# A two-layer trunk on one core: value and solution rows in one tile, products over 128 rows, small work off GpSimd, one projection a period ahead

## The chip, the cores and the metric

The kernel runs on one core of a Trainium2 chip. The metric is the device time of one execution in microseconds, the median of several runs. The engines are named as the profile names them: PE (TensorE, matrix products; PEld is its weight load), DVE (VectorE), ACT (ScalarE), POOL (GpSimd) and SP (SyncE, which issues most transfers). Each engine works through its own list of instructions in order and waits on semaphores for the others.

## What is computed

A trunk of two layers over 640 tokens (128 of a prompt, 512 of a sample, 1024 channels), with a norm and a conditioning in front of each layer and a last norm. The first layer holds a gated convolution and a bidirectional RWKV-7 recurrence over 16 heads of 64 channels; the second is gated linear attention. The change is in the first layer's recurrence and in what runs around it:

```python
def _wkv7_scan(r, w, k, kk, a, v, s0):
    def step(s, inp):
        r_t, w_t, k_t, kk_t, a_t, v_t = inp
        s_kk = jnp.einsum('zbhvk,zbhk->zbhv', s, kk_t)
        s = (s * w_t[..., None, :] - s_kk[..., :, None] * (kk_t * a_t)[..., None, :]
             + v_t[..., :, None] * k_t[..., None, :])
        return s, jnp.einsum('zbhvk,zbhk->zbhv', s, r_t)

w_raw = w0 + einsum(tanh(h @ w1), w2)                 # low-rank decay, two directions
decay = jnp.exp(-jnp.exp(-jax.nn.softplus(-w_raw) - 0.5))
o, s_fin = _wkv7_scan(r, decay, k_mod, kk, iclr, v, s0)   # forward and backward
gn = group_norm(o_fwd + o_bwd)
bonus = jnp.sum(rh[None] * k_mod * r_k, axis=(0, -1))[..., None] * vh
o_wkv = (gn + bonus) * jax.nn.silu(zw)
y = jnp.concatenate([o_conv, o_wkv], axis=-1) @ w_out
```

## The kernel before, in words

**Dense products.** Every projection (each head pair has its own 1024x128 block of every weight) is made as 128x320 products of split operands: each weight tile is split into a high part (ACT, L330) and a rest (POOL, L333), and three products hi·hi, lo·hi and hi·lo are summed. One projection is 48 such products of 320 tokens. In the rows they are `pd_...<-hi,hi_...`.

**The recurrence in chunks of 64 tokens.** Heads go in pairs, eight pairs, and each pair has its *period*. A period holds eight chain steps (`chain_step`, s = 0 to 7); a step treats two or three lanes (a lane is one chunk of one direction; 20 lanes a period, of which 18 update the state) for both heads h. A step has three stages on PE with `gap()` called twice behind each:

1. `x_mm` and `v_mm`: the right-hand side from the state X and the values V, into the PSUM tile `pa`; ACT copies it to `rh` (L994). Beside it POOL makes XP, the decayed state (L989).
2. `kv_mm`, `q_mm`, `gv_mm`: what V and X give to the new state and to the output, into `pu`; `t_mm`: the solution, from `rh`, into `pa`; ACT copies it with a minus to U (L1020).
3. `bk_start` (transposes of the next step's keys, copied to `bkt` by ACT, L941), then `bu_mm` and `gu_mm`: what U gives to state and output. DVE makes the new X (L1034), and the output goes to `oac` (L948 to L954).

V of head h lies in partitions HS[h], U of head h in the other half, HB[h], and all products of a step contract over 64 rows.

**What fills the gaps.** `Period.__call__`, run at every gap (48 a period), issues dense products by a quota and the small work (`Work`) that is due at this gap by the table PR: `p_lr` (low-rank decay of the pair after next: lw, ta), `p_kk` and `p_kb`, `expand_all` of the next pair (exponentials Pq and iP on ACT, products `ar` and `bk` on DVE L766 to L790, the pG products on PE and their masking on DVE L804), `inv_a` and `inv_b` (the triangular inversion, with a store to DRAM and a load), `vrows`, `bonus` (L856, L857), and of the pair before `fin_b` (DVE L1082) and `fin_t` (transposes pgn). `Work(p, g, n, first, last, ns, need)` spreads n pieces over the gaps first to last. The planner orders instructions on each engine by the priority in force when they were issued (PRE, CH, EV, FIN, BG).

**Period 7** has no next pair. Its dense work is the convolution's output projection (eoc), and DVE computes the second layer's conditioning (`gemv`, L247, into gacc; `gemv_cols` turns it to columns by one-column products pmod on PE).

In the table `en` a letter names the engine of each of twelve products E(0) to E(11): V is DVE and G is POOL.

Of the kernel before, what the change touches and what calls it, by code (L numbers as in the profile page):

```python
# [9 lines left out]
PR = {'NC0': 8,  # L10
# [16 lines left out]
 'ib': [42, 45],  # L27
# [5 lines left out]
 'ex': [1, 16],  # L33
 'inv': 17,
 'vr': 26,
 'bo': [28, 30],
 'lr': [34, 41],
 'kk': [40, 42],
 'init': 40,
 'fb': 10,  # L40
 'ft': [13, 16],
 'kb': [45, 46],
# [12 lines left out]
 'en': 'VVVVVGVVGVVV',  # L55
# [17 lines left out]
 'ex6': [1, 16],  # L73
 'inv6': 17,
# [3 lines left out]
 'fb6': 10,  # L78
 'ft6': [13, 16],
# [8 lines left out]
 'g49': [14, 39],  # L88
# [10 lines left out]
P = 128  # L99
# [28 lines left out]
def tile_trunk(ctx, tc, A, O):  # L128
# [318 lines left out]


# [216 lines left out]
    def p_lr(hp):  # L665
        w2h, w2l = {}, {}

        def load(i):
            w2 = wp.tile([P, 2, P], F32, tag="w2", name=f"w2_{hp}_{i}")
            nc.sync.dma_start(w2, A["w2"][hp, :, i])  # L670
            w2h[i] = wp.tile([P, 2, P], F32R, tag="w2h", bufs=2, name=f"w2h_{hp}_{i}")
            x = S.activation(w2h[i], w2, AF.Copy)
            if hp == 0 and i == 1:
                tc.keep_in_program_order(x)
            return w2

        def low(i, w2):

            w2l[i] = wp.tile([P, 2, P], F32R, tag="w2l", name=f"w2l_{hp}_{i}")
            G.tensor_tensor(w2l[i], w2, w2h[i].bitcast(F32), op=ALU.subtract)  # L680
        low(1, load(1))
        raw0 = load(0)
        yield 0
        lw, ta = [], []
        for (lst, i, boff, tg) in ((ta, 1, 16, "ta"), (lw, 0, 0, "lw")):
            if not i:
                low(0, raw0)
                lwt = el.tile([P, 2, TOK], F32, tag="lw", name=f"lw{hp}")
            for d in range(2):
                o = et(f"{tg}{d}", f"{tg}{hp}_{d}") if i else lwt[:, d]  # L690
                b = der[:, boff + d * 8 + hp:boff + d * 8 + hp + 1]
                for s in range(2):
                    ps = pm(f"plr{hp}_{d}_{tg}_{s}")
                    t = slice(s * HT, (s + 1) * HT)
                    mm(ps[:, 0:HT], w2h[i][:, d], hlr[i, d][:, t], start=True, stop=False)
                    mm(ps[:, 0:HT], w2l[i][:, d], hlr[i, d][:, t], start=False, stop=True)
                    evict(lambda: S.activation(o[:, t], ps[:, 0:HT], AF.Tanh, scale=0.5, bias=b))
                    yield 270
                lst.append(o)
        for d in range(2):  # L700
            S.activation(lw[d], lw[d], AF.Identity, scale=-0.5 * CW, bias=mcw)
            for t in (slice(0, HT), slice(HT, TOK)):
                m, x = cc("sm", HT, d), lw[d][:, t]
                if d == 1:
                    m, x = m[:, ::-1], x[:, ::-1]
                V.tensor_tensor_scan(x, m, x, 0.0, op0=ALU.mult, op1=ALU.add)
        st[hp].update(lw=lw, ta=ta)

    def p_kk(hp):
# [4 lines left out]
        for t in (slice(0, HT), slice(HT, TOK)):  # L714
            S.activation(kk[:, t], k[:, t], AF.Square, scale=pc("kk", hp))
# [31 lines left out]
    def expand(hp, d, c0):  # L747
# [16 lines left out]
        if d == 0:  # L764
            E(11).tensor_tensor(ar[:, :, 1, 1:], kk3[:, :, 1:], P3[:, :, :-1], op=ALU.mult)
            V.tensor_copy(ar[:, :, 1, 0:1], kk3[:, :, 0:1])  # L766
            end = P3[:, :, C - 1]
            if c0 == 0:
                V.tensor_copy(PC[:, 0:2, 2], end[:, 0:2])
                V.tensor_copy(PC[:, 0:3, 0], end[:, 2:5])  # L770
            else:
                V.tensor_copy(PC[:, 3:8, 0], end)
        else:
            E(11).tensor_tensor(ar[:, :, 1, 1:][:, :, ::-1], kk3[:, :, :-1], P3[:, :, 1:], op=ALU.mult)
            V.tensor_copy(ar[:, :, 1, 0:1], kk3[:, :, C - 1:C])
# [16 lines left out]
    def pairs(hp, d, c0, m):  # L792
# [100 lines left out]
    def inv_b(hp):  # L893
# [3 lines left out]
        T = et("r", f"Tb{hp}").rearrange("p (c x) -> p c x", x=B)  # L897
# [23 lines left out]
    def chain_init(hp):  # L921
# [3 lines left out]
        oac = wk.tile([P, NCH, 64], F32, tag="oac", bufs=2, name=f"oac{hp}")  # L925
        st[hp]["X"], st[hp]["oac"] = X, oac
# [29 lines left out]
    def chain_step(hp, s, gap):  # L956
# [12 lines left out]
        if s == 0:  # L969
            bk_start(hp, 0, ta)  # L970
# [18 lines left out]
        dict(V=V, G=G)[PR["xpc"]].tensor_tensor(XP[:, l0:nl], X[:, l0:nl], PC[:, s, l0:nl].unsqueeze(2).to_broadcast([P, nl - l0, 64]), op=ALU.mult)  # L989
# [7 lines left out]

        begun = set()

        def kv_mm(l, d, c, h):  # L1000
            mm(po[HS[h], 0, l], bt[HS[h], l, 64 * h:64 * h + 64], Vt[HS[h], c], start=h not in begun, stop=False, skip_group_check=True)
            begun.add(h)

        def q_mm(l, d, c, h):
            if full(l):
                mm(po[HS[h], 1, l], ar[HS[h], d, c, 0], X[HS[h], l], start=False, stop=False, skip_group_check=True)

        def gv_mm(l, d, c, h):
            mm(po[HS[h], 1, l], Gt[h][HS[h], d, c, 0:C], Vt[HS[h], c], start=False, stop=False, skip_group_check=True)
# [112 lines left out]
    class Work:  # L1122
# [147 lines left out]
    def period(hp):  # L1270
# [7 lines left out]
        if n < NHP:  # L1278
# [4 lines left out]
            misc += [Work(PRE, expand_all(n), 8, *(PR["ex" + z] if hp else PR["ex0"]), 540, (n, "r"))]  # L1283
# [620 lines left out]
```

## Time and profile before

| what | value |
|---|---|
| median of 3 runs | 1467.71 us (1459.54 to 1475.93) |
| the profiled execution | 1467.22 us |
| its span | 1465.5 us |
| mean granted clock of PE | 0.944 |
| busy: PE, DVE, ACT, POOL | 92%, 67%, 43%, 35% |
| periods | eight, about 107 us each, from 191.5 to 1070 us; period 7 from 943 us |

A busy share is over the whole span. The page's chain of work that ended last goes by PE for 45% and by DVE for 34%. The stages differ: inside a period there is a stretch in which the next pair's operands are expanded, with other limits than the rest, so the periods are read by windows below. A record is what the profiler logs; one product of 64x64 in 32 bits shows as two records.

### The profile page before, as it was taken

Reading aid. Unit: us, or ns where it says so; the run is one execution under the profiler, and the core shown is the slowest. Engines: PE = TensorE matmul, PEld = TensorE weight load, DVE = VectorE, ACT = ScalarE, POOL = GpSimd, SP = SyncE. Lnnn points to the kernel's source line nnn. Section 1 sums busy time; section 2 is a strip of 40 time slices with the busy share of each in tenths; the row PEclk is TensorE's granted clock in tenths of the full one; section 3 lists DMA queues with packets and bytes.
Section 4 is the critical chain, followed back from the end, with each engine's and each line's share of the span. In section 5 each row is a group of like instructions: output and inputs, shape, how many; then the busy total and the mean of one; then the engine's idle time right before and its main releaser. Section 6 shows DMA issues by size and latency. Waiting matters only on the chain.

```text
span 1465.5 us, 34615 instructions
## 1 busy us (share of the span) xinstructions
PE 1353.6 (92%) x13495; PEld 1240.8 (85%) x13495; DVE 981.3 (67%) x2283; ACT 630.8 (43%) x1574; POOL 519.3 (35%) x675
## 2 busy tenths in 40 slices
PE   9889899999999999898999989888999999999997
PEld 4779788888888888887888878878989888999997
DVE  4386556785876786685686787675775687746454
ACT  4543253454444444444444533442344664344341
POOL 1433233323323333233223223443355444343332
PEclk9989999999999999899999989997889999999998
DMA  9112212212212212212212212455544321422143
GB/s 367 38 51 82 78 45 66 71 39 74 65 46 63 66 50 65 56 42 72 56 43 71 64 55 62 118 184 165 163 116 131 110 72 53 124 73 89 56 130 102
DMA packets 139636, 127.28 MB, mean 87 GB/s; under 512 B 54096, under 2 KB 121936, under 8 KB 139472
## 3 DMA queue, kind: packets, MB, share of 16 engines
q1 hardware_dynamic: 136912, 118.38, 27.3%
q0 software_dynamic: 2016, 6.16, 1.1%
q8 instruction: 106, 1.74, 0.5%
q14 instruction: 58, 0.48, 0.1%
q10 hardware_dynamic: 544, 0.52, 0.1%
HBM read 108.37 MB, written 16.65 MB: 85 GB/s over the span
## 4 chain that ended last, share of the span: by engine, by line
PE 45%; DVE 34%; DMA 7%; issue 4%; POOL 3%; ACT 2%; SPq 0%; DVEq 0%; POOLq 0%; ACTq 0%
DVE Ai L881 6%; DVE Ai L879 6%; PE pd_oo L135 3%; PE pd_zg L135 3%; PE pu L135 3%; PE pd_eoc L135 3%; PE pd_gb L135 3%; PE pd_r L135 3%; DVE bk L790 3%; PE pd_v L135 3%; PE pd_qk L135 2%; PE pd_vg L135 2%; DVE bk L787 2%; DMA gw<-in_ada_dram 2%; PE pd_u L135 2%
## 5 line engine op out<-in xcount | busy, mean ns | idle before, releaser
L879 DVE TENSOR_TENSOR Ai<-Ai 80x30 f32<-80x30 f32 (+14 forms) x240 | 96.5, 402 | 22.8 <-DMA Ai<-Ad 15.5
L881 DVE TENSOR_TENSOR Ai<-Ai 80x30 f32<-80x30 f32 (+14 forms) x240 | 100.1, 417 | 6.9
L135 PE MATMUL pG<-ar,bk 64*128 64x128 f32 x640 | 66.4, 320 | 27.7 <-DVE G L804 15.3
L135 PEld LDWEIGHTS pG<-ar,bk 64*128 64x128 f32 x640 | 52.3, 212 | 40.4 <-DVE G L804 17.2
L804 DVE TENSOR_TENSOR G<-pG,con 128x512 f32<-128x512 f32 (+1 forms) x96 | 53.1, 594 | 26.1 <-PE pG L135 25.8
L247 DVE SCALAR_TENSOR_TENSOR gacc<-gw,cf,gacc 128x512 f32<-128x512 f32 x70 | 59.9, 895 | 15.3 <-DMA gw<-in_ada_dram 15.1
L1034 DVE SCALAR_TENSOR_TENSOR X<-pu,PC,XP 128x64 f32<-128x64 f32 x144 | 33.1, 275 | 51.9 <-POOL lo_k L333 27.6
L989 POOL TENSOR_TENSOR XP<-X,PC 128x128 f32<-128x128 f32 (+2 forms) x56 | 30.3, 542 | 101.0 <-DVE X L1034 85.5
L333 POOL TENSOR_TENSOR lo_eoc<-wr_eoc,hi_eoc 128x256 fp32r<-128x256 f32 x48 | 40.2, 846 | 50.9 <-ACT hi_eoc L330 30.9
L333 POOL TENSOR_TENSOR lo_r<-wr_r,hi_r 128x256 fp32r<-128x256 f32 x32 | 25.2, 791 | 82.0 <-ACT hi_r L330 81.4
L1020 ACT ACTIVATE U<-pa 128x192 f32<-128x192 f32 (+1 forms) x64 | 19.3, 302 | 77.9 <-PE pa L135 77.9
L994 ACT ACTIVATE rh<-pa 128x192 f32<-128x192 f32 (+1 forms) x64 | 19.2, 300 | 65.5 <-PE pa L135 65.5
L135 PE MATMUL pd_eoc<-hi,hi_eoc 128*128 128x320 f32 x128 | 45.5, 356 | 1.0 <-ACT hi_eoc L330 1.0
L135 PE MATMUL pd_eoc<-hi,lo_eoc 128*128 128x320 f32 x128 | 44.0, 343 | 2.5 <-POOL lo_eoc L333 2.5
L790 DVE TENSOR_TENSOR bk<-ta,iP 64x320 f32<-64x320 f32 x64 | 44.4, 693 | 1.4
L135 PE MATMUL pd_gb<-hi,hi_gb 128*128 128x320 f32 x128 | 43.4, 339 | 0.7 <-DVE cy L619 0.7
L135 PE MATMUL pd_eoc<-lo,hi_eoc 128*128 128x320 f32 x128 | 43.4, 339 | 0.4 <-POOL lo L1207 0.4
L135 PE MATMUL pd_gc<-hi,hi_gc 128*128 128x320 f32 x128 | 43.7, 342 | 0.0
L135 PE MATMUL pd_gc<-hi,lo_gc 128*128 128x320 f32 x128 | 43.7, 341 | 0.0
L135 PE MATMUL pd_gc<-lo,hi_gc 128*128 128x320 f32 x128 | 43.2, 338 | 0.0
L135 PE MATMUL pd_r<-hi,hi_r 128*128 128x320 f32 x128 | 42.3, 331 | 0.6 <-ACT hlr L583 0.6
L135 PE MATMUL pd_gb<-hi,lo_gb 128*128 128x320 f32 x128 | 42.4, 331 | 0.0
(484 smaller groups left out, 5096.8 us busy)
## 6 DMA issues: line engine op xcount, KB each, us to landing
gw<-in_ada_dram SPq DMA_DIRECT2D x64, 256.0 KB, 3.1
gw<-in_ada_dram SPq DMA_DIRECT2D x16, 512.0 KB, 8.6
wr_eoc<-in_eo_dram SPq DMA_DIRECT2D x48, 128.0 KB, 2.8
wr_qk<-in_ow_dram SPq DMA_DIRECT2D x33, 128.0 KB, 2.2
wr_r<-in_ew_dram SPq DMA_DIRECT2D x32, 128.0 KB, 2.4
wr_v<-in_ew_dram SPq DMA_DIRECT2D x32, 128.0 KB, 2.2
wr_u<-in_ew_dram SPq DMA_DIRECT2D x32, 128.0 KB, 2.2
wr_gc<-in_ew_dram SPq DMA_DIRECT2D x32, 128.0 KB, 2.2
```

The lines of the kernel that those rows point to most:

```text
L135: tc.keep_in_program_order(T.matmul(*a, **kw))
L247: V.scalar_tensor_tensor(acc[j], w, c, acc[j], op0=ALU.mult, op1=ALU.add)
L333: le.tensor_tensor(lo, w, hi.bitcast(F32), op=ALU.subtract)
L787: V.scalar_tensor_tensor(x if d == 0 else x[:, :, ::-1], b13[HS[h]], 0.5, iP3[HS[h]], op0=ALU.mult, op1=ALU.mult)
L790: E(2).tensor_tensor(bk[HS[h], :, h], ta3[HS[h]], iP3[HS[h]], op=ALU.mult)
L804: V.tensor_tensor(q["G"][h][:, d, c0:c0 + m], ps[h][:, 0:P * m].rearrange("p (c x) -> p c x", x=P), cc("mk", P, 256 * h + P * d).unsqueeze ...
L879: V.tensor_tensor(tt, Ai[:, 0:i, i:i + 1].to_broadcast([80, i, n]), Ai[:, i:i + 1, i + 1:].to_broadcast([80, i, n]), op=ALU.mult)
L881: V.tensor_tensor(Ai[:, 0:i, i + 1:], Ai[:, 0:i, i + 1:], tt, op=ALU.add)
L989: dict(V=V, G=G)[PR["xpc"]].tensor_tensor(XP[:, l0:nl], X[:, l0:nl], PC[:, s, l0:nl].unsqueeze(2).to_broadcast([P, nl - l0, 64]), op=ALU.mult)
L994: S.activation(rh[:, 0:nl], pr[:, 0:nl], AF.Copy)
L1020: S.activation(U[:, 0:nl], pr[:, 0:nl], AF.Copy, scale=-1.0)
L1034: V.scalar_tensor_tensor(Xn[:, l], po[:, 0, l], PC[:, s, l:l + 1], XP[:, l], op0=ALU.mult, op1=ALU.add)
```

## The change

**One tile for V and U.** A step now has a tile VU with V of head h in partitions HS[h] and minus the solution in HB[h]. ACT copies V's part (two operations, four where a step has three lanes) and writes the solution's part in two operations of 64 partitions. `kv_mm` and `bu_mm` become one `s_mm`, `gv_mm` and `gu_mm` one `o_mm`, both contracting over 128 rows, both in stage 3.

**Work off GpSimd and DVE.** XP is made by ACT, one operation a lane. The products E(5) (gn by sz) and E(8) (the bonus) go from POOL to DVE. The ten small copies a pair in the expansion (L766 to L781) go from DVE to ACT.

**Places.** The projection r of a pair is made a period earlier (at the end of the dense list; v stands first). `inv_b` keeps its T in the tile that will be `oac`, no longer in r's. The transposes for step 0 of the next pair are issued in step 7 of this one. `p_lr(0)` starts ahead of ten dense products in the prologue. The table's gaps change: expansion [1, 16] to a list of eight gaps, inversion 17 to 14, `fin_b` 10 to 14 and `fin_t` 13-16 to 17-20, `p_lr` 34-41 to 39-47, `p_kk` 40-42 to 38-40, `ib` 42-45 to 44-47, `gemv_cols` [14, 39] to [18, 46]; `Work` accepts a list of gaps. `fin_s` goes from priority EV+600 to PRE+100, `load_wkv(0)` from BG to EV, and the squares of kk are issued through `evict`.

```diff
- 'ex': [1, 16],
+ 'ex': [0, 1, 5, 7, 9, 11, 12, 13],
- 'en': 'VVVVVGVVGVVV',
+ 'en': 'VVVVVVVVVVVV',
...
-            V.tensor_copy(ar[:, :, 1, 0:1], kk3[:, :, 0:1])
+            S.activation(ar[:, :, 1, 0:1], kk3[:, :, 0:1], AF.Copy)
...
-        T = et("r", f"Tb{hp}").rearrange("p (c x) -> p c x", x=B)
+        oac = st[hp]["oac"] = wk.tile([P, NCH, 64], F32, tag="oac", bufs=2, name=f"oac{hp}")
+        T = oac.rearrange("p a x -> p (a x)").rearrange("p (c x) -> p c x", x=B)
...
-        if s == 0:
+        if s == 0 and hp == 0:
             bk_start(hp, 0, ta)
...
-        dict(V=V, G=G)[PR["xpc"]].tensor_tensor(XP[:, l0:nl], X[:, l0:nl], PC[:, s, l0:nl].unsqueeze(2).to_broadcast([P, nl - l0, 64]), op=ALU.mult)
+        for l in range(l0, nl):
+            S.activation(XP[:, l], X[:, l], AF.Copy, scale=PC[:, s, l:l + 1])
...
+        VU = wk.tile([P, 2, 3, 64], F32, tag="VU", name=f"VU{hp}_{s}")
+        a, b = 2 + s, 9 - s
+        for h in range(2):
+            if a < b:
+                S.activation(VU[HS[h], h, 0:2], Vt[HS[h], a:b + 1:b - a], AF.Copy)
...
+            if nl == 3:
+                S.activation(VU[HS[h], h, 2], Vt[HS[h], lanes[2][2]], AF.Copy)
...
-        each(kv_mm, upd)
         each(q_mm, lanes)
-        each(gv_mm, lanes)
         each(t_mm, lanes)
         gap()
         gap()
-        U = wk.tile([P, 3, 64], F32, tag="U", name=f"U{hp}_{s}")
-        S.activation(U[:, 0:nl], pr[:, 0:nl], AF.Copy, scale=-1.0)
...
-        bk_start(hp, s + 1, ta)
-        each(bu_mm, upd)
-        each(gu_mm, lanes)
+        for h in range(2):
+            S.activation(VU[HB[h], h, 0:nl], pr[HB[h], 0:nl], AF.Copy, scale=-1.0)
+
+        def s_mm(l, d, c, h):
+            mm(po[HS[h], 0, l], bt[:, l, 64 * h:64 * h + 64], VU[:, h, l], start=False, stop=False, skip_group_check=True)
+
+        def o_mm(l, d, c, h):
+            mm(po[HS[h], 1, l], Gt[h][:, d, c, 0:C], VU[:, h, l], start=False, stop=l == nl - 1, skip_group_check=True)
+        if s < 7 or hp < 7:
+            bk_start(hp + s // 7, (s + 1) % 8, ta)
+        each(s_mm, upd)
+        each(o_mm, lanes)
...
-            dense_ += [(PRE, p_r(n)), *conv_next(a), (PRE, p_v(n)), *conv_next(b)]
+            dense_ += [(PRE, p_v(n)), *conv_next(a)]
...
-                dense_ += [(PRE, p_k(n + 1))]
+                dense_ += [(PRE, p_k(n + 1)), *conv_next(b), (PRE, p_r(n + 1))]
```

The order of the instructions moves in three places.

On PE, stage 2 of a step with two lanes (step 2 of period 7), before the change; `pu` is the step's PSUM tile for state and output, `pa` that of the solution, and G_0 and G_1 are the two heads' operands:

```order
L135 MATMUL pu_2_12752<-V_11816,bkt_2_12659 64x64 x4
L135 MATMUL pu_2_12752<-X_1_12744,ar_11144 64x64 x4
L135 MATMUL pu_2_12752<-V_11816,G_0_11146 64x64
L135 MATMUL pu_2_12752<-V_11816,G_1_11147 64x64
L135 MATMUL pu_2_12752<-V_11816,G_0_11146 64x64
L135 MATMUL pu_2_12752<-V_11816,G_1_11147 64x64
L135 MATMUL pa_2_12751<-rh_2_12782,G_0_11146 64x64
L135 MATMUL pa_2_12751<-rh_2_12782,G_1_11147 64x64
```

On PE, the only products on values that the changed step keeps behind its solution are these, in stage 3:

```order
L138 MATMUL pa_2_12495<-con,bk_10766 128x128 x2
L135 MATMUL pu_2_12496<-VU_2_12529,bkt_2_12403 64x64 x4
L135 MATMUL pu_2_12496<-VU_2_12529,G_0_10767 64x64
L135 MATMUL pu_2_12496<-VU_2_12529,G_1_10768 64x64
L135 MATMUL pu_2_12496<-VU_2_12529,G_0_10767 64x64
L135 MATMUL pu_2_12496<-VU_2_12529,G_1_10768 64x64
```

The eight products on V left stage 2, and stage 3 has as many as before, now on VU; stage 2 keeps those on X and rh.

On DVE, the end of the expansion phase (the last `bk` of a pair, which PE's last pG products need), before; `pG` are the products to be masked, `cv` belongs to the convolution, `oac` is the output of the pair before:

```order
L804 TENSOR_TENSOR G_0_9695<-pG_0_8_0_9860,con 128x256
L804 TENSOR_TENSOR G_1_9696<-pG_0_8_1_9861,con 128x256
L787 SCALAR_TENSOR_TENSOR bk_9694<-Pq_1_5_9830,iP_1_5_9831 64x5x64 x2
L788 TENSOR_TENSOR ta_1_9076<-ta_1_9076,k_8875 128x320
L1082 TENSOR_TENSOR oac_7714<-oac_7714,gst 128x320
L804 TENSOR_TENSOR G_0_9695<-pG_1_0_0_9891,con 128x512
L804 TENSOR_TENSOR G_1_9696<-pG_1_0_1_9892,con 128x512
L856 TENSOR_TENSOR ta_0_9005<-ta_0_9005,ta_1_9076 128x640
L631 TENSOR_TENSOR cv_9197<-pd_gb_1_9845,cv_9197 128x320
L790 TENSOR_TENSOR bk_9694<-ta_1_9076,iP_1_5_9831 64x5x64 x2
```

On DVE, the same place after the change:

```order
L806 TENSOR_TENSOR G_0_9340<-pG_0_8_0_9635,con 128x256
L806 TENSOR_TENSOR G_1_9341<-pG_0_8_1_9636,con 128x256
L857 TENSOR_TENSOR ta_0_8988<-ta_0_8988,ta_1_9033 128x640
L1037 SCALAR_TENSOR_TENSOR X_1_9692<-pu_1_9515,PC_7915,XP_1_9528 128x64 x3
L858 TENSOR_TENSOR r_8712<-ta_0_8988,r_8712 128x640
L790 TENSOR_TENSOR bk_9339<-ta_1_9033,iP_1_0_9493 64x5x64
L213 TENSOR_TENSOR rst_9309<-rsy_9308 128x10
L214 SCALAR_TENSOR_TENSOR rst_9309<-rst_9309,gst 128x10
L215 SCALAR_TENSOR_TENSOR gst<-rst_9309,rsy_9308 128x10
L787 SCALAR_TENSOR_TENSOR bk_9339<-Pq_1_5_9585,iP_1_5_9586 64x5x64 x2
```

The bonus product (L858) is now on DVE, ahead of three of the last `bk` products, and `fin_b`'s L1082 has left this stretch.

On PE in period 7, the first of the one-column products on DVE's sums gacc_ta (gemv_cols), before:

```order
L135 MATMUL pa_2_12751<-rh_2_12782,G_1_11147 64x64
L135 MATMUL pd_eoc_0_12732<-hi_103,hi_eoc_0_12716 128x320
L135 MATMUL pd_eoc_0_12732<-lo_104,hi_eoc_0_12716 128x320
L135 MATMUL pd_eoc_0_12732<-hi_103,lo_eoc_0_12717 128x320
L135 MATMUL pmod_12803<-one,gacc_ta_12487 128x1
```

On PE, the same product after the change:

```order
L135 MATMUL pa_3_12597<-V_11487,G_0_10767 64x64
L135 MATMUL pa_3_12597<-V_11487,G_1_10768 64x64
L135 MATMUL pd_eoc_1_12556<-lo_104,hi_eoc_0_12460 128x320
L135 MATMUL pd_eoc_1_12556<-hi_103,lo_eoc_0_12461 128x320
L135 MATMUL pmod_12612<-one,gacc_ta_12236 128x1
```

It moved from stage 2 of step 2 to stage 1 of step 3, two stages later.

## Rows read from the trace of the kernel before

**Rows 1.** The page, part 1: busy us, share of span, instructions

```profile
PE 1353.6 (92%) x13495; PEld 1240.8 (85%) x13495; DVE 981.3 (67%) x2283; ACT 630.8 (43%) x1574; POOL 519.3 (35%) x675
```

**Rows 2.** Windows: us; busy PE, PEld, DVE, ACT, POOL; PEclk, DMA, GB/s

```profile
300.00:943.00 643.00, 595.77 (x7637) 541.36 (x7637) 466.12 (x1207) 286.06 (x728) 204.12 (x279) 0.95 0.22 61
735.50:773.00 37.50, 33.41 (x382) 29.93 (x381) 33.21 (x85) 17.03 (x41) 11.91 (x15) 0.91 0.16 44
943.00:1070.00 127.00, 116.25 (x1081) 107.63 (x1078) 88.88 (x135) 43.98 (x107) 52.31 (x56) 0.85 0.56 168
993.80:1010.80 17.00, 15.06 (x69) 13.96 (x69) 9.56 (x15) 2.48 (x7) 2.88 (x4) 0.50 0.42 131
```

**Rows 3.** PE's waits, 300 to 943 us: us in total, times, longest us

```profile
PE pG L135 <- DVE G L804: 12.0, 7, 2.3
PE pgn L138 <- DVE oac L1082: 8.6, 3, 4.4
PE pss L135 <- ACT lw L697: 6.1, 3, 3.7
PE pa L135 <- ACT bkt L941: 5.3, 7, 1.0
PE pG L135 <- DVE bk L790: 5.0, 6, 1.3
...
PE pa L135 <- ACT rh L994: 0.5, 1, 0.5
```

**Rows 4.** Timeline of PE, a step: start us, us, engine, line, shapes, records

```profile
708.31 0.56 PE L135 MATMUL pu<-V,bkt 64*64 64x64 f32 x12
...
708.94 0.52 PE L135 MATMUL pu<-V,G 64*64 64x64 f32 x12
709.29 0.52 PE L135 MATMUL pa<-rh,G 64*64 64x64 f32 x12
...
711.31 0.31 PE L135 MATMUL pd_zw<-hi,hi_zw 128*128 128x320 f32 x1
711.46 0.31 PE L135 MATMUL pd_zw<-lo,hi_zw 128*128 128x320 f32 x1
```

**Rows 5.** Timeline of PE, prologue: the products over 128 rows and 32 columns

```profile
25.22 1.06 PE L135 MATMUL pgv<-gw,cfz 128*32 128x512 f32 x8
26.21 0.45 PE L135 MATMUL first<-hi,hi_first 128*128 128x384 f32 x1
```

**Rows 6.** Timeline of DVE, expansion phase; in brackets idle before, releaser

```profile
750.28 0.79 DVE L782 TENSOR_TENSOR ar<-r,Pq 128x320 f32<-128x320 f32 x1 [1.17 <-ACT r L446]
...
753.17 0.49 DVE L790 TENSOR_TENSOR bk<-ta,iP 64x320 f32<-64x320 f32 x1
...
770.31 2.36 DVE L790 TENSOR_TENSOR bk<-ta,iP 64x320 f32<-64x320 f32 x2
```

**Rows 7.** Groups of DVE, 300 to 943: busy, mean ns | idle, releaser

```profile
L790 DVE TENSOR_TENSOR bk<-ta,iP 64x320 f32<-64x320 f32 x48 | 34.9, 726 | 1.1
...
L706 DVE TENSOR_TENSOR_SCAN lw<-con,lw 128x320 f32<-128x320 f32 x20 | 16.4, 846 | 4.5 <-ACT lw L701 4.5
...
L766 DVE COPY ar<-kk 128x5 f32<-128x5 f32 x12 | 7.6, 665 | 0.0
...
L1082 DVE TENSOR_TENSOR oac<-oac,gst 128x320 f32<-128x320 f32 x12 | 7.4, 625 | 0.2
```

**Rows 8.** Groups of POOL, whole span, as in Rows 7

```profile
L989 POOL TENSOR_TENSOR XP<-X,PC 128x128 f32<-128x128 f32 (+2 forms) x56 | 30.3, 542 | 101.0 <-DVE X L1034 85.5 <-PE pd_r L135 8.4 <-PE pd_eoc L135 2.4
```

**Rows 9.** Groups of ACT by form, 729 to 836 us, as in Rows 7

```profile
L1020 ACT ACTIVATE U<-pa 128x192 f32<-128x192 f32 x4 | 1.3, 327 | 3.7 <-PE pa L135 3.7
...
L952 ACT ACTIVATE oac<-pu 128x64 f32<-128x64 f32 x2 | 0.4, 217 | 0.0
```

**Rows 10.** PE's waits, 943 to 1070 us, as in Rows 3

```profile
PE pmod L135 <- DVE gacc L247: 5.2, 3, 3.3
```

**Rows 11.** PE's waits, 0 to 90 us, as in Rows 3

```profile
PE plr_ta L135 <- ACT w2h L672: 5.2, 1, 5.2
```

More of the change, by code (lines that the diff above doesn't have):

```diff
@@ L77 @@
  'init6': 43,
[L78 to L79 removed]
+ 'fb6': 14,
+ 'ft6': [17, 20],
  'kb6': [2, 3],
@@ L446, in evac_act, with p_lr, load, low @@
         return lambda ps, t: S.activation(dst[:, t], ps, func, **kw)
+    def p_lr(hp):
+        w2h, w2l = {}, {}
+        def load(i):
+            w2 = wp.tile([P, 2, P], F32, tag="w2", name=f"w2_{hp}_{i}")
+            nc.sync.dma_start(w2, A["w2"][hp, :, i])
+            w2h[i] = wp.tile([P, 2, P], F32R, tag="w2h", bufs=2, name=f"w2h_{hp}_{i}")
+            S.activation(w2h[i], w2, AF.Copy)
+            return w2
+        def low(i, w2):
+            w2l[i] = wp.tile([P, 2, P], F32R, tag="w2l", name=f"w2l_{hp}_{i}")
+            G.tensor_tensor(w2l[i], w2, w2h[i].bitcast(F32), op=ALU.subtract)
+        low(1, load(1))
+        raw0 = load(0)
+        yield 0
+        lw, ta = [], []
+        for (lst, i, boff, tg) in ((ta, 1, 16, "ta"), (lw, 0, 0, "lw")):
+            if not i:
+                low(0, raw0)
+                lwt = el.tile([P, 2, TOK], F32, tag="lw", name=f"lw{hp}")
+            for d in range(2):
+                o = et(f"{tg}{d}", f"{tg}{hp}_{d}") if i else lwt[:, d]
+                b = der[:, boff + d * 8 + hp:boff + d * 8 + hp + 1]
+                for s in range(2):
+                    ps = pm(f"plr{hp}_{d}_{tg}_{s}")
+                    t = slice(s * HT, (s + 1) * HT)
+                    mm(ps[:, 0:HT], w2h[i][:, d], hlr[i, d][:, t], start=True, stop=False)
+                    mm(ps[:, 0:HT], w2l[i][:, d], hlr[i, d][:, t], start=False, stop=True)
+                    evict(lambda: S.activation(o[:, t], ps[:, 0:HT], AF.Tanh, scale=0.5, bias=b))
+                    yield 270
+                lst.append(o)
+        for d in range(2):
+            S.activation(lw[d], lw[d], AF.Identity, scale=-0.5 * CW, bias=mcw)
+            for t in (slice(0, HT), slice(HT, TOK)):
+                m, x = cc("sm", HT, d), lw[d][:, t]
+                if d == 1:
+                    m, x = m[:, ::-1], x[:, ::-1]
+                V.tensor_tensor_scan(x, m, x, 0.0, op0=ALU.mult, op1=ALU.add)
+        st[hp].update(lw=lw, ta=ta)
     new_h()
@@ L552, in tile_trunk @@
                 ahead["r0", q] = weights(A["ew"][32], "r0", q)
+            lr0 = p_lr(0)
+            next(lr0)
             prio(1)
@@ L663, in p_v @@
         st[hp]["ok"] = st[hp].get("ok", "") + "v"
[L665 to L707, printed above, removed]
     def p_kk(hp):
@@ L1128, in want @@
         def want(self, gap):
+            if isinstance(self.first, (list, tuple)):
+                return sum(g <= gap for g in self.first)
             w = self.last - self.first + 1
@@ L1136, in upto @@
             if gap < 1000:
-                want = min(want, self.done + -(-self.n // (self.last - self.first + 1)))
+                want = min(want, self.done + (1 if self.last is None else -(-self.n // (self.last - self.first + 1))))
             while self.done < want or (self.done >= self.n and self.g is not None):
@@ L1310, in tile_trunk @@
     prio(PRE)
-    lr0 = p_lr(0)
-    next(lr0)
     w1 = [] if PR["lr1"] else [Work(PRE, p_lr(1), 9, *PR["plr1"], 270, (0, "b"))]
```

82 lines of the change are left out of this document (39 added, 43 removed).

## The prediction

> **What bounds the kernel now.** I read the page's busy line first: TensorE (PE) is busy 92% of the profiled execution, VectorE (DVE) 67%, ScalarE (ACT) 43%, GpSimd (POOL) 35% [rows 1]. So time leaves this kernel in two ways only: PE gets less to do, or PE waits less. The windows come next [rows 2]: in the six periods from 300 to 943 us, 107 us each, PE is busy 595.8 of 643 us at a granted clock of 0.95. Since the clock has two levels, 2.4 and 1.2 GHz, 0.95 means a tenth of that stretch, 64 us, at half clock. Period 7 (943 to 1070) stands at 0.85. The stretch 735.5 to 773 is another kind of stage: it is the expansion of the next head pair's operands, DVE is busy 33.2 of its 37.5 us, and PE's clock is 0.91. There DVE sets the end and PE waits. Last, PE's waits in the six periods [rows 3]: pG on DVE (12.0 and 5.0, the expansion), pgn on oac (8.6), pss on lw (6.1), pa on bkt (5.3, once at each period's start). The chain's own waits, for rh and U, are next to nothing: 0.5 us. Behind the longest wait in the program, 3.3 us for gacc in period 7 [rows 10], stand 17 us at half clock [rows 2]: a wait costs more than its length.
>
> **The change, part by part**, against the profiled execution, 1467.2 us (the median of the three runs is 1467.7, so the sum stands for either).
>
> *A. Products over 128 rows.* Each period has 20 lanes with two heads in the output product and 18 in the state product: 76 products over V's 64 rows and 76 over U's. They become 76 over 128 rows, 608 products fewer in eight periods. A product here is two records (a step with three lanes has six and shows x12), and records run two by two: the start of one x12 group to the next is 0.35 us, so 58 ns a pair of records, or 116 ns for a pair of products [rows 4]. 304 pairs of products by 0.116 is **-35.3 us**, if products of 128x64 also run two by two. No row has such a product. The nearest is pgv: all 128 rows by 32 columns, eight records of 512 columns in 0.99 us from its start to the next row's [rows 5]. One after the other, at the rate of 64 columns in 0.058, they would take 8 x 0.46 = 3.7 us: there four run side by side. So products that differ in columns alone do run beside each other, and I take the whole gain; the other bound is 0 (if they run one by one, each costs what a pair costs today).
>
> The Trainium skill, "TensorEngine Tiling (Array Packing)", section Tiling Modes, lists four tiles of 64x64 and two of 128x64. Read alone it speaks against this change: four old products at a time would cost what two new ones do, so A would be 0 and the sum 35 us higher. The trace shows two at a time, not four, in a program that has issued them by rows and columns together.
>
> *B. The next pair's first transposes* (bk_start of step 0) go from the period's start, where the first state product waits for their copy, into step 7 of the period before: the seven waits for bkt are gone, **-5.3**. In place of them three transposes stand ahead of step 7's last products, where the operands have been ready for a stage. If DVE's bk came late they would hold the chain there; but bk is done at 772.7 [rows 6], and step 7 of that period runs after 820. The bound is 0.
>
> *C. Later places for small work.* fin_b moves from gap 10 to 14 with its transposes (13-16 to 17-20), p_lr from 34-41 to 39-47 while the inversion starts at 14 for 17. The wait of pgn for oac (8.6) and that for lw (6.1, ACT holding its queue for the inversion's store) are 14.7; I take **-12**, with 0 and -20 as bounds, for later work can be late again.
>
> *D. The expansion phase.* Up to its last pG product PE has 103 dense products in place of 119 (16 by the 0.147 between two starts [rows 4], 2.4), 40 step products fewer (20 pairs, 2.3), and five pgn transposes that now come behind (0.5): 5.2 us less to hide DVE's work. DVE's list changes by: four scans of 0.85 that were done before the period (+3.4 [rows 7]); the bonus product off GpSimd, 640 columns, at twice the 0.49 of 320 columns [rows 6] less the overlap of starts (+0.9); ten small copies to ACT (L766 alone 7.6 in six periods, 1.3 each; I take 2.3 for all ten); fin_b's two products behind the phase (-1.2 [rows 7]); no wait for r, now made a period ahead (-1.2 [rows 6]); a start one gap earlier, 107/48 (-2.2); less collision with GpSimd (-0.8). This last: L790 takes 0.49 alone and 2.36 for two beside GpSimd [rows 6], 0.726 on the mean [rows 7], so eight a period lose 1.9, and GpSimd gives up its XP and bonus products in just this phase; I take four tenths. Together DVE ends 3.4 earlier, PE has 5.2 less: PE waits 1.8 longer, six times, **+11**. If DVE's end stays where it is, +31; if the collisions vanish and more copies were on the way, -6.
>
> The Trainium skill, "SBUF — State Buffer", section Who interferes with whom, says a DVE instruction with two SBUF inputs shuts out a GpSimd instruction that reads SBUF, and the reverse. The trace agrees in kind (0.49 against 1.2 a piece). By that rule, whole, the 1.9 would go too.
>
> *E. Half clock.* 64 us at half clock cost up to 32 us; B and C take away some 17 of the 37 us of waits in [rows 3] but D adds 11: **-4**, bounds 0 and -15.
>
> *F. Period 7.* The products on gacc come two stages later (gap 14 to 18). Their waits, 5.2 [rows 10], and the half clock: 0.85 over 127 us is 38 us at half, up to 19 lost. I take **-10**, bounds 0 and -20.
>
> *G. Front.* The first w2 load goes ahead of ten dense products; the wait for it is 5.2 [rows 11]. What would end next there is the low-rank operand, made in the same microseconds: **-1**, bounds 0 and -5.
>
> *H. ScalarE.* 60 more operations a period: XP 18, V copies 24, U 8, small copies 10. From 0.217 (128x64) to 0.327 (128x192) each [rows 9], 13 to 20 us, some 14.5; ACT goes from 631 to about 747 us. The cover: a chain stage is followed by 12 to 14 dense products, 1.8 to 2 us, and PE waits for rh 0.5 us in all. **0**. Uncovered, U's second half alone costs 64 by 0.327, 21 us.
>
> At nothing I cost: DVE's products gn*sz off GpSimd, which lie beside PE's dense work (uncovered, seven at 0.9, 6 us); the inversion's T in the tile of the next oac, which is a second buffer and free from gap 20 on, while T is written at 44; kk's square, fin_s and load_wkv at another priority, beside dense work too. Sum: -35.3 - 5.3 - 12 + 11 - 4 - 10 - 1 = -56.6, so 1467.2 - 56.6 = **1411 us**.
>
> **Rivals.** *1. ScalarE's queue takes GpSimd's wait.* XP needs X of the step before; GpSimd now stands idle for it 85.5 us over 56 operations, 1.5 each [rows 8]. On ACT rh, U, evictions and the weight splits stand behind XP. If half of those waits reach PE: 1411 + 43 = 1454, no change. If all do: 1411 + 85.5 = 1496, slower. It decides for "slower by over 1%" from 71 us on, 1.3 us a step. For it: ACT runs in order and its work grows by a fifth. Against: X has been made before x_mm of the next step starts, and XP is written behind x_mm in the program, with ACT idle half of its time.
> *2. 128x64 products don't pair.* A is 0: 1446. The page's rule leads to the same time. Against it: pgv [rows 5].
> *3. DVE's end does not move.* D is +31, and with it E and F bring nothing: 1411 + 20 + 14 = 1445.
> *4. GpSimd's relief is worth more.* D is -6: 1394.
> *5. The change doesn't do what it says*: r a period ahead removes waits that are DVE's, not PE's. That is 1.2 a period, inside D.
>
> **How the numbers follow.** Forecast 0.38 (1411, its own range 1397 to 1428), rival 4 0.11, rival 2 0.08, rival 3 0.15, rival 1 by half 0.18, in full 0.10. About 1% (1453 and 1482) is what a measurement of this kernel can tell from no change. Faster: 0.38 + 0.11 + 0.08 + 0.15 = 0.72; same 0.18; slower 0.10. The range 1390 to 1462 leaves out rival 1 in full (0.10), the upper third of its half (0.06) and the end of rival 4 (0.03).
>
> **What would show it.** A: groups of pu<-VU start 0.35 us apart at x12 (six products) and the step has two groups fewer; 0.7 apart would be rival 2. B: no wait for bkt at a period's start. C: the oac and lw rows are gone from PE's waits. D: PE's waits for G and bk together stand near 28 us in six periods, 17.0 now; over 45 is rival 3, under 12 rival 4. F: the clock in period 7 is above 0.90. H and rival 1: PE's waits for rh, U and VU; over 20 us means that ACT holds the chain. Wrong would be the whole sum if PE's busy time fell by 35 us and the span didn't: then the chain, not PE's work, had set the pace between the phases.

## The result, and the profile after

| kernel | median | runs | ratio to before (95% interval) |
|---|---|---|---|
| before | 1463.86 us | 4 | 1 |
| changed | 1424.05 us (1419.71 to 1428.28) | 4 | 0.9715 (0.9646 to 0.9784) |

The change makes the kernel 2.8% faster. The forecast was 1411 us, with 1390 to 1462 as its range: the sign was right, and 13 us too much was promised. The experiments below show that the sum came out near partly by luck: some of its terms were too favourable, one was far too small.

What follows is read from one profiled execution of each kernel, 1465.5 and 1422.5 us long: 43 us apart, where the medians are 40 apart. The page after; the columns are those of [rows 1]:

```profile
PE 1307.4 (92%) x12279; PEld 1193.4 (84%) x12279; DVE 960.6 (68%) x2218; ACT 739.0 (52%) x2054; POOL 461.8 (32%) x596
```

PE has 1216 records fewer, the 608 products of step A, and 46 us less busy time; ACT has 108 us more (116 were forecast), POOL 57 less. Next the windows (as in [rows 2]): first the seven periods 0 to 6 of the kernel before, whole, which start where a step on X_i starts,

```profile
192.50:937.90 745.40, 692.64 (x8764) 630.75 (x8764) 539.31 (x1376) 330.72 (x844) 236.97 (x322) 0.95 0.22 61
```

and then the same seven of the changed kernel, and one expansion of it:

```profile
190.80:905.90 715.10, 656.71 (x7698) 590.64 (x7698) 517.84 (x1313) 422.89 (x1258) 183.80 (x251) 0.96 0.23 62
707.20:743.00 35.80, 30.78 (x326) 27.10 (x325) 29.47 (x68) 19.20 (x61) 9.87 (x13) 0.94 0.16 45
```

Of the 43 us, 30 come from the periods 0 to 6. Period 7 and what follows it up to the first product of the output projection (pd_eow) gives 9, from 163.8 to 154.7 us by the starts of those products, the prologue 2. The expansion is still DVE's, which is busy 29.5 of its 35.8 us, and its end moved forward as forecast: the last bk product of the period that starts at 707.2 us ends 31.5 us after that start,

```profile
738.21 0.49 DVE L790 TENSOR_TENSOR bk<-ta,iP 64x320 f32<-64x320 f32 x1
```

where in the kernel before it ended 36.1 us after the start of the same period (772.7 by [rows 6], 736.6). PE's waits for bk in the seven periods were, before,

```profile
PE pG L135 <- DVE bk L790: 8.9, 9, 2.0
```

and those for G as in [rows 3]. PE's waits in the seven periods of the changed kernel (as in [rows 3]):

```profile
PE pG L135 <- DVE bk L790: 16.8, 15, 1.8
PE pG L135 <- DVE G L806: 7.2, 5, 2.5
PE pa L138 <- ACT VU L1022: 4.4, 3, 1.8
PE pT L135 <- DVE oac L902: 4.3, 2, 4.0
PE pd_k L135 <- ACT k L446: 3.8, 5, 1.1
PE pa L135 <- DVE X L1037: 3.8, 5, 1.5
PE pd_zc L135 <- DVE cv L683: 2.5, 1, 2.5
...
PE pa L135 <- ACT bkt L942: 1.4, 1, 1.4
```

The waits for fin_b's oac (at pgn) and for lw (at pss) of [rows 3] are gone, those for bkt nearly. The oac in the row of pT is another matter: it is the inversion's T, which now lies in that tile. New are the waits of dense products (pd_...), which the kernel before did not have in these periods. Added over all projections they are 21.0 us in the changed kernel; three of the larger stand here.

The step, on PE's timeline (as in [rows 4]), two lanes, in the kernel before the products on U,

```profile
700.80 0.45 PE L135 MATMUL pu<-U,bkt 64*64 64x64 f32 x8
701.08 0.40 PE L135 MATMUL pu<-U,G 64*64 64x64 f32 x8
```

and in the changed kernel those on VU:

```profile
648.27 0.45 PE L135 MATMUL pu<-VU,bkt 128*64 128x64 f32 x8
648.55 0.40 PE L135 MATMUL pu<-VU,G 128*64 128x64 f32 x8
```

Eight records at the head of such a series take 0.28 us from start to start over 64 rows and over 128 rows: those of 128x64 run two by two, at the same price. So the price in step A was right. (With three lanes the first group takes 0.40 us in both kernels; the 0.35 named as the sign is that of a group further behind.) Whether 304 pairs of them are worth 35 us is another question.

### The profile page after: what moved, and what is told of

The parts are those of the page before. It is cut to its first block, busy times and chain, and to the rows that moved or that the text cites. A ratio compares the mean times of both kernels' runs of the same rounds, so it can differ in the third digit from the quotient of the medians.

```text
span 1422.5 us, 32431 instructions
## 1 busy us (share of the span) xinstructions
PE 1307.4 (92%) x12279; PEld 1193.4 (84%) x12279; DVE 960.6 (68%) x2218; ACT 739.0 (52%) x2054; POOL 461.8 (32%) x596
## 4 chain that ended last, share of the span: by engine, by line
PE 45%; DVE 26%; ACT 4%; DMA 4%; issue 4%; POOL 1%; SPq 0%; POOLq 0%; DVEq 0%; ACTq 0%
PE pd_zg L135 4%; PE pd_oo L135 4%; PE pd_zw L135 3%; PE pd_qk L135 3%; PE pd_k L135 3%; DVE Ai L882 3%; PE pu L135 3%; PE pd_zc L135 3%; DVE Ai L880 2%; PE pd_eoc L135 2%; PE pd_gc L135 2%; PE pa L135 2%; DVE gacc L247 2%; PE pd_vg L135 2%; DVE bk L790 2%
## 5 line engine op out<-in xcount | busy, mean ns | idle before, releaser
L1022 ACT ACTIVATE VU<-pa 64x192 f32<-64x192 f32 (+1 forms) x128 | 38.3, 299 | 55.0 <-PE pa L135 53.8
L333 POOL TENSOR_TENSOR lo_gc<-wr_gc,hi_gc 128x256 fp32r<-128x256 f32 x32 | 27.8, 876 | 70.9 <-ACT hi_gc L330 70.1
L333 POOL TENSOR_TENSOR lo_gb<-wr_gb,hi_gb 128x256 fp32r<-128x256 f32 x32 | 25.4, 800 | 73.5 <-ACT hi_gb L330 44.4
L333 POOL TENSOR_TENSOR lo_zw<-wr_zw,hi_zw 128x256 fp32r<-128x256 f32 x32 | 27.2, 861 | 62.7 <-ACT hi_zw L330 56.3
L991 ACT ACTIVATE XP<-X,PC 128x64 f32<-128x64 f32 x120 | 35.8, 342 | 21.1 <-DVE X L1037 20.8
L135 PE MATMUL pd_zc<-hi,hi_zc 128*128 128x320 f32 x128 | 42.7, 334 | 4.3 <-DVE cv L683 2.5
L333 POOL TENSOR_TENSOR lo_zc<-wr_zc,hi_zc 128x256 fp32r<-128x256 f32 x32 | 24.8, 781 | 65.3 <-ACT hi_zc L330 60.6
L333 POOL TENSOR_TENSOR lo_u<-wr_u,hi_u 128x256 fp32r<-128x256 f32 x32 | 26.8, 840 | 59.2 <-ACT hi_u L330 56.8
L135 PE MATMUL pd_k<-hi,hi_k 128*128 128x320 f32 x112 | 37.3, 333 | 9.4 <-ACT k L446 3.8
L333 POOL TENSOR_TENSOR lo_k<-wr_k,hi_k 128x256 fp32r<-128x256 f32 x28 | 23.5, 841 | 65.1 <-ACT hi_k L330 63.8
```

Of the source, the lines that this page charges most:

```text
L135: tc.keep_in_program_order(T.matmul(*a, **kw))
L333: le.tensor_tensor(lo, w, hi.bitcast(F32), op=ALU.subtract)
L991: S.activation(XP[:, l], X[:, l], AF.Copy, scale=PC[:, s, l:l + 1])
L1022: S.activation(VU[HB[h], h, 0:nl], pr[HB[h], 0:nl], AF.Copy, scale=-1.0)
```

## The experiments

All ratios are to the kernel before on the same chip. "Periods" are 0 to 6, from the first X_i product to that of period 7; "idle" is their length less PE's busy time. "Theory" and "rival" are the two expectations of a run.

**Merge alone.** The kernel before with VU, s_mm and o_mm; bk_start, gaps, engines and projections as before.

```diff
-        each(kv_mm, upd)
...
-        each(gv_mm, lanes)
...
-        each(bu_mm, upd)
-        each(gu_mm, lanes)
+        each(s_mm, upd)
+        each(o_mm, lanes)
```

> The kernel before with one part of the change alone: V and minus U in one tile, state and output products over 128 rows. Theory (PE's work is what ends last, products of 128x64 run two by two): 608 products fewer at 0.058 us each, 35 us, and nothing else moved, so about 1430 us, 0.976 of before; the groups of products on VU start 0.28 us apart for eight records, as those on V and U did. Rival (the copies of V and the solution's second half on ScalarE hold the chain, or PE only waits longer for VectorE): PE's busy time falls by 35 us but its waits rise, 1445 to 1460 us, 0.985 to 1.0 of before.

Measured: 1471.5 us, 1.0066 (1.0042 to 1.0090): slower by 10 us. PE's windows and waits in its periods:

```profile
193.50:942.00 748.50, 671.78 (x7698) 608.15 (x7698) 533.98 (x1376) 385.56 (x1068) 233.78 (x322) 0.93 0.21 60
```

```profile
PE pss L135 <- ACT lw L697: 16.4, 5, 4.5
PE pG L135 <- DVE bk L790: 14.4, 12, 2.4
PE pG L135 <- DVE G L804: 11.3, 6, 2.2
PE pgn L138 <- DVE oac L1083: 11.1, 6, 3.6
PE pT L135 <- DVE Tb L900: 8.8, 7, 4.5
```

PE is busy 21 us less than before in the periods, although 31 us of products are gone (1064 records, 532 pairs by 0.058): what is left runs slower, at 0.93 in place of 0.95. And the periods are 3 us longer. The waits at pss, pgn and pT, the products that need lw, fin_b's oac and the inversion's T, went from 20 to 42 us. The run with merge and gaps (below) shows that the places of the small work are at fault, for there these waits fall to 3 us. How they arise is argued. ACT waits for the store of the inversion's matrix Ai, which shares its buffers with lw, as long as it did, in the merge-only kernel and in the kernel before:

```profile
ACT lw L697 <- DMA Td<-Ai: 16.8, 5, 3.8
ACT lw L697 <- DMA Td<-Ai: 16.7, 4, 4.9
```

Small work is placed by counting gaps, and less of PE's work now lies between two gaps, while DVE's inversion, its store and its load are as long as they were.

**Gaps alone.** The kernel before with the changed table's gaps (those ahead of the periods too, with one piece of the convolution less there), and nothing else.

```diff
- 'inv': 17,
+ 'inv': 14,
...
- 'lr': [34, 41],
+ 'lr': [39, 47],
...
- 'ft': [13, 16],
+ 'ft': [17, 20],
```

> The kernel before with the new gaps of the small work alone: products over 64 rows, all engines and the list of projections as before. Merge and gaps together gave 0.973 of before, the merge alone 1.007. Theory (PE's work sets the pace as soon as the small work isn't late, so the merge is worth its 31 us in the periods once the gaps fit): the waits for decay, inversion and fin_b fall from 20 to under 6 us in periods 0 to 6, and the time is 1450 to 1460 us, 0.99 to 1.0 of before, so that the merge on top of it gives 25 us or more. Rival (the gaps alone carry the gain, and the merge brings next to nothing beside them): 1425 to 1438 us, 0.973 to 0.98 of before.

Measured: 1457.6 us, 0.9940 (0.9904 to 0.9975), in the theory's band. The profile is of the fastest of its ten runs, 1452.0 us. PE's window and waits in its periods:

```profile
190.20:934.20 744.00, 688.31 (x8810) 628.27 (x8810) 550.66 (x1374) 334.19 (x850) 232.94 (x326) 0.97 0.22 61
```

```profile
PE pa L135 <- DVE X L1034: 20.2, 16, 2.4
PE pG L135 <- DVE G L804: 18.1, 12, 2.6
PE pa L135 <- ACT bkt L941: 13.0, 7, 2.2
PE pG L135 <- DVE bk L790: 4.7, 9, 0.7
```

The waits at pss, pgn and pT are gone, and the periods are no shorter (744.0 and 745.4): the chain waits instead, for X 20.2 and bkt 13.0. What the gaps gain alone lies mostly in period 7: 163.8 to 151.4 us up to pd_eow, by the later gemv_cols.

**Merge and gaps.** Both edits, nothing else.

> The kernel before with two parts of the change: the merged products and the new gaps of the small work, nothing else. The merge alone gave 1.007 of before with PE's waits in periods 0 to 6 up from 53 to 77 us, most of it for the decay (pss), the inversion (pT) and fin_b (pgn). Theory (the shorter PE work brings each gap earlier in time, so small work placed by gaps comes due before VectorE, the inversion's store and its load are done; later gaps mend that): pss, pT and pgn together fall from 42 to under 15 us, 1430 to 1445 us, 0.98 to 0.99 of before. Rival (ScalarE's extra copies hold everything up): those waits stay over 25 us and the time stays within 0.5% of before or above it.

Measured: 1425.9 us, 0.9731 (0.9712 to 0.9750), better than the theory's band, and within the interval of the whole change. Its waits in the periods:

```profile
PE pa L135 <- DVE X L1035: 17.3, 14, 2.0
PE pG L135 <- DVE G L804: 16.6, 10, 2.5
PE pa L135 <- ACT bkt L941: 12.2, 8, 1.8
PE pG L135 <- DVE bk L790: 8.3, 11, 1.7
PE pT L135 <- DVE Tb L900: 2.9, 8, 1.1
```

With the gaps in place the merge is worth 31 us (0.9940 to 0.9731), without them it costs 10. ScalarE's extra copies are in both kernels with the merge, so they are not what held the merge alone back. These two parts reach by themselves what the whole change reaches; the rest of it adds up to nothing that the intervals tell, and the runs below show why.

**The changed kernel without the merge.** Products over 64 rows put back, all else changed.

> The changed kernel with the products over 64 rows put back (V's products in stage 2, U's in stage 3, one operation for U and no copies of V); everything else stays changed. Theory (the merge is worth 35 us wherever it stands): 1459 us, 1.025 of the changed kernel, about 0.997 of before. Rival (the merge is worth less here, since the 14.5 us a period that it and the other moves add on ScalarE come back as waits): 1440 us or less, 0.985 of before or less, and the waits of dense products on ScalarE's evictions, 21 us in the periods of the changed kernel, fall by half or more.

Measured: 1435.3 us, 0.9824 (0.9792 to 0.9856). Beside the two measurements of the changed kernel (0.9715 and 0.9693) the merge is worth 16 to 19 us there, with 5 to 29 allowed by the intervals: less than 35, and not surely less than the 31 above (25 to 37). The rival's number held, its reason did not: the dense products' waits are 19.7 us in the periods, nearly the 21.0 of the changed kernel, with fewer copies on ScalarE. As with the merge alone, a part of the saved work comes back: without the merge PE is idle 46 us in the periods at a clock of 0.98, with it 58 us at 0.96.

**The changed kernel with the old gaps.**

> The changed kernel with the gaps of the small work (expansion, inversion, fin_b and fin_t, p_lr, p_kk, p_kb, gemv_cols) put back to those of before. Theory (the later gaps took away the waits for oac and lw, 14.7 us, and part of period 7's): 1424 + 12 + 5, about 1440 us, 0.984 of before, with waits of pgn for oac and pss for lw back in the trace. Rival (the new gaps only moved the waits, to dense products whose evictions stand behind fin_t's copies): 1424 within 7 us, the dense products' waits for k gone and as much back at pgn and pss.

Measured: 1451.2 us, 0.9933 (0.9906 to 0.9959), further off than the theory said: the gaps are worth 32 to 35 us in the changed kernel, where alone they were worth 9. (The places ahead of the periods and in the first expansion stay the changed ones.) In the periods the waits at pss are back at 12.3 us and those at pT stand at 12.3; in period 7

```profile
PE pmod L135 <- DVE gacc L247: 10.4, 2, 7.7
```

Its periods are 18 us longer than the changed kernel's (733.2 and 715.1), and period 7 up to pd_eow 8.6 us.

**The changed kernel with the engines put back.** XP, bonus and gn by sz on POOL, the ten small copies on DVE.

```diff
- 'en': 'VVVVVVVVVVVV',
+ 'en': 'VVVVVGVVGVVV',
...
```

> The changed kernel with the small work put back on the engines of before: XP, the bonus product and gn by sz on GpSimd, the ten small copies on VectorE. Theory (ScalarE's additions are hidden, VectorE's expansion gains from GpSimd's relief): 1424 + 3 to 10, about 1431 us, 0.978 of before, and PE's waits for bk and G in the periods grow over 24 us. Rival (ScalarE's queue takes as much as it gives): with some 8 us a period less on ScalarE the waits of dense products on its evictions and of the chain on VU, 21 and 4 us, go down by 10 or more, 1410 to 1415 us, 0.965 of before.

Measured: 1448.3 us, 0.9909 (0.9883 to 0.9936). The theory's direction, at about three times the upper end of its 3 to 10 us: 28 to 32 us by the ratios. PE's waits in the periods:

```profile
PE pG L135 <- DVE bk L790: 17.9, 13, 3.0
PE pG L135 <- DVE G L806: 16.9, 7, 4.1
PE pa L135 <- DVE X L1036: 14.4, 15, 1.9
```

bk and G together 34.8 in place of 24.0, X 14.4 in place of 3.8.

**r in its own period.** The changed kernel with the list of projections of before.

```diff
-            dense_ += [(PRE, p_v(n)), *conv_next(a)]
+            dense_ += [(PRE, p_r(n)), *conv_next(a), (PRE, p_v(n)), *conv_next(b)]
...
-                dense_ += [(PRE, p_k(n + 1)), *conv_next(b), (PRE, p_r(n + 1))]
+                dense_ += [(PRE, p_k(n + 1))]
...
```

> The changed kernel with the list of dense projections of before: r of a pair in its own period, ahead of the expansion that needs it. Theory one (r a period ahead takes 1.2 us of VectorE's idle time a period and no more): 1424 + 7, with VectorE's waits for r back in the expansion. Theory two (the new list is what makes PE wait 21 us for the eviction of the half projection it has just finished, waits that neither the kernel before nor the merge alone shows): those waits fall under 5 us and the time is 1405 to 1418 us, 0.96 to 0.97 of before.

Measured: 1409.5 us, 0.9624 (0.9592 to 0.9657): theory two, and **faster than the changed kernel**, whose runs all lie above all of these. Its periods take 705.0 us. PE's waits there:

```profile
PE pG L135 <- DVE G L806: 16.5, 8, 2.7
PE pa L135 <- DVE X L1037: 9.1, 9, 2.0
PE pG L135 <- DVE bk L790: 8.8, 10, 1.9
PE pa L138 <- ACT VU L1022: 5.0, 5, 1.7
```

Not one of them is a dense product's. DVE waits 3.4 us for r again in the periods, and that is hidden. How such a wait looks in the changed kernel, on ACT's timeline and then on PE's:

```profile
548.12 0.42 ACT L446 ACTIVATE k<-pd_k 128x320 f32<-128x320 f32 x1
548.44 0.34 ACT L991 ACTIVATE XP<-X,PC 128x64 f32<-128x64 f32 x1
```

```profile
547.60 0.31 PE L135 MATMUL pd_k<-hi,lo_k 128*128 128x320 f32 x1
548.59 0.41 PE L135 MATMUL pd_k<-hi,hi_k 128*128 128x320 f32 x1 [0.69 <-ACT k L446]
```

The first product of k's second half starts 0.05 us after ACT has copied out the first half (548.12 + 0.42 = 548.54). Three tiles of PSUM, the memory that PE writes its sums to and that ACT or DVE must copy out, serve the halves; here the new half waits for the one just finished. That the planner gave it the same tile is argued from this; why it does so with this list and not with the old one stays open. A version that names the three tiles in turn was not tried.

**The same, twice more.** r in its own period and one product back on POOL: the bonus, and XP.

> The changed kernel with r in its own period (1410 us, 0.962 of before) and the bonus product alone put back on GpSimd. Theory (on VectorE it costs 0.9 us a period in the stretch that holds the last pG products, on GpSimd it shuts out VectorE's products for 1.7 us): 2 to 8 us slower, 0.964 to 0.968 of before. Rival (VectorE's list is what counts, the collision little): 2 to 8 us faster, PE's waits for G and bk under 22 us in place of 25.

> The changed kernel with r in its own period and the decayed state XP alone put back on GpSimd. Theory (XP on GpSimd is late for VectorE's new state, and stands in the way of VectorE's products): PE's waits for X rise from 9 to 15 us or more, 5 to 12 us slower, 0.966 to 0.971 of before. Rival (ScalarE's 5 us a period for XP cost as much as they bring): within 4 us of 1410, waits for X as they were.

> The changed kernel itself, for a comparison on the same chip as the two runs with r in its own period. Theory (r a period ahead costs some 14 us, the waits for the half projection just finished): 1424 us, 0.972 of before, with 20 us of waits of dense products in periods 0 to 6. Rival (the difference between the two was one of chips): within 4 us of the others.

Measured: bonus on POOL 1415.4 us, 0.9651 (0.9596 to 0.9706), in the theory's band but not told apart from 0.9624. XP on POOL 1423.6 us, 0.9708 (0.9652 to 0.9764): 12 us slower by the ratios, at the end of the theory's band, but not by its first reason: PE's waits for X rose only from 9.1 to 10.9, those for G from 16.5 to 20.9. The changed kernel once more: 1420.7 us, 0.9693 (0.9635 to 0.9751), with 20.9 us of dense waits in the periods. So r a period ahead costs 10 us beside this measurement on the same chip, and 13 beside the first one. DVE's bk product in the periods, as a group (as in [rows 7]), in the changed kernel, then with r in its own period, then with r in its own period and XP on POOL, then the changed kernel with all engines put back:

```profile
L790 DVE TENSOR_TENSOR bk<-ta,iP 64x320 f32<-64x320 f32 x56 | 33.2, 593 | 0.9
```

```profile
L790 DVE TENSOR_TENSOR bk<-ta,iP 64x320 f32<-64x320 f32 x56 | 29.5, 526 | 1.2
```

```profile
L790 DVE TENSOR_TENSOR bk<-ta,iP 64x320 f32<-64x320 f32 x56 | 36.2, 647 | 1.2
```

```profile
L790 DVE TENSOR_TENSOR bk<-ta,iP 64x320 f32<-64x320 f32 x56 | 40.9, 730 | 1.0
```

XP alone lengthens the bk products by 6.7 us in the periods, and DVE's busy time there by 12.6 (534.5 and 521.9). But the engines are not all that sets this mean: in the kernel before it was 0.706 us over the same seven periods, and with merge and gaps, where all engines are those of before,

```profile
L790 DVE TENSOR_TENSOR bk<-ta,iP 64x320 f32<-64x320 f32 x56 | 34.4, 615 | 1.1
```

**Two small ones.** V's copies left out, so that V's part of state and output is missing, and in another kernel the first transposes back at the period's start.

> The changed kernel with ScalarE's copies of V into the tile left out: the tile is cleared once and keeps zeros in V's rows, so V's part of state and output is missing; all products run as before. 24 operations a period, some 6 us of ScalarE. Theory (ScalarE's additions are hidden, as the prediction cost them at 0): within 5 us of the changed kernel, 1419 to 1429 us, 0.97 of before. Rival (they stand ahead of evictions and of the decayed state, and so hold PE): 1400 to 1412 us, 0.96 of before, PE's waits for dense evictions down by 8 or more.

> The changed kernel with the first transposes of a pair back at the period's start. Theory (the seven waits for bkt at the period's start come back, 1.0 us each and the clock behind them): 1424 + 5 to 8, about 1430 us, and no waits of the transposes for VU in step 7. Rival (the move only changed what PE waits for, the transposes in step 7 wait 4.4 us for VU in three places): 1424 within 3 us.

Measured: without the copies 1417.8 us, 0.9678 (0.9652 to 0.9704); with the transposes back 1428.0 us, 0.9744 (0.9722 to 0.9766). Beside 0.9715 (0.9646 to 0.9784) and 0.9693 neither is told apart from the changed kernel: 2 to 5 us for the copies and 4 to 7 for the transposes, by ratios whose intervals overlap. With the transposes back PE's waits for bkt are 12.2 us in the periods, for 1.4, and those for VU are gone. The rival read these as waits of step 7. They are not: the three of the changed kernel stand in step 0, 8 us after a period's start. One of them, on ACT's timeline and then on PE's:

```profile
410.49 0.42 ACT L455 ACTIVATE w2h<-w 128x256 fp32r<-128x256 f32 x1 [2.52 <-DMA w<-in_w_dram]
411.29 0.66 ACT L1022 ACTIVATE VU<-pa 64x192 f32<-64x192 f32 x2
```

```profile
412.00 0.55 PE L138 MATMUL pa<-con,bk 128*128 128x128 f32 x3 [1.80 <-ACT VU L1022]
```

Here ACT waited 2.5 us for the load of p_lr's weights from DRAM, with VU's copy behind that operation in its list; at the other two places it waited 2.1 and 2.0 us.

## Why the prediction was right, and where its steps were wrong

Taken in one order, each run beside the one with a part less, in microseconds of a kernel of 1465: gaps -9, merge -31, engines, transposes and the rest -16, r a period ahead +10 to +13. The sum, -43 to -46, is the whole change by construction. In another order the parts are worth something else, as the runs on the changed kernel show.

- **A (-35) was right in price and wrong as a term by itself.** Two by two and 0.28 us for eight records, as forecast; rival 2 is out. The page "TensorEngine Tiling (Array Packing)" of the Trainium skill, section Tiling Modes, lists four tiles of 64x64. No run here shows four products at once, and none tests it: in the kernel before, a group of products puts each head's half of the rows to one half of the columns, so it uses two of the four quarters. But the work that A takes off PE is worth +10, -31 or -16 to -19 us, by what stands around it. The step assumed that PE's work ends last everywhere outside the expansion; where small work hung on a count of gaps it did not.
- **C (-12) and F (-10).** C's waits did go, all of them, and in the kernel before that brought the periods 1.4 us: the chain's waits for X and bkt took their place. C's worth is mostly what it lets A bring. F was right in size: -12 in the run with the gaps alone (163.8 to 151.4), 8.6 in the changed kernel, one profile each; the changed kernel's second profile has 150.8 where its first has 154.7. The sign named for it, a clock above 0.90 in period 7, was missed in the first profile (0.89, from 0.85) and met in the second (0.95).
- **B (-5.3).** The waits for bkt fell to 1.4, and in step 7 the transposes wait for nothing, as the step said. Its worth isn't told apart from 0.
- **D (+11).** DVE's last bk came 4.6 us earlier in the period shown, 3.4 were forecast, and PE's waits for G and bk grew from 20.9 to 24.0 in seven periods, 3 us. (The sum took it six times; seven periods have an expansion.) Which term of D's long list made the difference stays open; the waits are 24.9 already with merge and gaps, before any engine is changed. The relief of L790 from GpSimd, put at 0.8 us a period, is 1.1 by the run that differs in the engines alone (0.730 to 0.593 us, eight a period). Page "SBUF — State Buffer", section Who interferes with whom, of the Trainium skill says that a VectorE instruction with two SBUF inputs contends with a GpSimd instruction that reads SBUF; these means agree with it. But D saw only the expansion. The engines' move as a whole is worth 28 to 32 us in the changed kernel, far more than the 13 that D's terms for it (+0.9, -2.3 and -0.8 a period, six times) come to: with the engines put back PE also waits 14.4 us for X in place of 3.8.
- **The step that failed is r a period ahead**, costed inside D as a gain of 1.2 us a period. The wait it removes was DVE's, 12.1 us in the periods before, and was covered; its list of projections brought PE 21 us of waits for evictions, the copies out of PSUM. It was costed as a change of date; it also changed which half follows which.
- **E (-4).** The clock went from 0.95 to 0.96 in the periods: 75 us at half clock became 57, worth some 9. **G (-1)**: the prologue is 1.7 us shorter. **H (0)**: ACT's 108 us are hidden, but for the 2 to 5 us that V's copies may cost and the 4.4 us that PE waits for VU while ACT waits for p_lr's weights. **Rival 1** did not happen: PE's waits for X are 3.8, for rh 0.6 us.

The forecast of 1411 is met almost to the microsecond by the kernel without r's move, 1409.5. That is luck: A and r were put too favourably, the engines' move too low, and these errors nearly cancel.

## What to carry to other kernels

Taking work off the busiest engine cost 10 us here where other work was timed by it, and gained 31 where that work had been moved too. If small work is placed by counting steps, shorten the steps and move the counts in one edit, and measure the four corners, since each edit alone may show a loss or next to nothing. When a list of products is reordered, look at which buffer the first product of each group waits for; here a move that freed a covered wait cost 10 us more than it freed.

## What the hardware showed that was not expected

PE ran slower with less to do: with the merge alone its clock in the periods fell from 0.95 to 0.93 and it stood idle 77 us in place of 53; the changed kernel has 0.96 with the merge and 0.98 without. The sum of the idle time does not decide it: with the gaps alone PE was idle 56 us, more than before, and its clock was 0.97. Its longest single wait was then 2.6 us, where it was 4.4 us before and 4.5 us with the merge alone; that the long waits make the difference is not shown. A small product of GpSimd (XP, 128 partitions by 64 or 128) made a VectorE product of 320 columns 0.12 us longer on the mean of 56.
